# Mixers of a two-layer hybrid trunk in another order: mLSTM beside the later projections, attention last and alone

## The chip, the cores and the metric

The kernel runs on one core of one Trainium2 chip. The metric is the device time of one launch in microseconds (us). Three runs of the kernel before gave a median of 1076.05 us (1075.78 to 1082.33).

## The reference, cut to what matters

Two layers (DEPTH = 2) over x of 512 rows and D_MODEL = 1024. In each layer three mixers read one input projection, their heads go side by side through one output projection, and a normalisation and a mixture of experts follow:

```
p = einsum('bsd,dc->bsc', x, w_in[l])
(c_q, c_kv, k_r, m_q, m_k, m_v, m_o, m_g, s_z, s_xbc, s_dt) = _split(p, IN_SIZES)
y_a = _mla(c_q, c_kv, k_r, ...)               # 8 heads: softmax(q k^T) v, latents of 256 and 128
y_b = _mlstm(m_q, m_k, m_v, m_o, m_g, ...)    # 4 heads of 64, both directions, then a norm and an output gate
y_c = _ssd(s_z, s_xbc, s_dt, ...)             # 4 heads of 64, state 128, both directions
heads = concatenate([y_a, y_b, y_c], -1)      # 512 + 256 + 256 columns
x = _layernorm(ALPHA * x + heads @ w_out[l], ...)
x = _layernorm(ALPHA * x + _hier_moe(x, ...), ...)   # 16 experts, group top-1, expert top-2
```

mLSTM's end is `hn = (h - mu) * rsqrt(var + 1e-5) * norm_g` over each head's 64 columns, times `sigmoid(o)`. The three mixers do not need each other; the output projection needs all three.

## The kernel before, in words

**Numbers.** Products run as three matmuls of split operands (`mm3`: high by high, high by low, low by high). x lies transposed in SBUF (`xt`), 8 blocks of 128 columns; the mixers' finished heads are written back into the same blocks (`finish_heads`, an ACTIVATE and a DVE operation on `xt`): attention into blocks 0 to 3, mLSTM 4 and 5, SSD 6 and 7.

**Stages of one layer.** Layer 0 takes about 60 to 285 us for the mixers, layer 1 about 591 to 815 us.
- `ssd()` (the letter d, 19 steps): the SSD's scans on 128-row chunks; `ssd_heads()` (h) its heads.
- `projections()` (p, 12 steps): the input projection's blocks for mLSTM q and k, then the two attention latents (`cqb`, `ckb`), then mLSTM v (`mvb`) and the output gate (`tho`). Their weights are loaded in the order of `todo_w` (L715), two blocks ahead.
- `mla_in()` (i): norms of the latents, v of attention.
- `mlstm()` (m, 16 steps): four heads in two pairs; products of 130 and 65 columns; at the end, all on the vector engine DVE, mean (`mu`), difference, variance (`va`), a reciprocal root of 16 columns by some 14 small operations (`rq_*`), two 1024-column products and two 512-column products with the gate; then eight 128x128 transposes into banks 3 and 4 and the heads into `xt`. This end is called the mLSTM's tail below.
- `attention()`: generators `scores` (s, 5 steps a head) and `values` (v). A score tile is three matmuls of 512 columns into one bank, a DVE maximum (`mx`), an ACT exponential with its sum (`sums`), a DVE reciprocal and a normalisation (L1337; on POOL for heads 0 to 5, on DVE for 6 and 7). `values` transposes four 128x128 blocks into one bank, copies them out, and multiplies with v (64 x 512 outputs).

**What sets the order.** The string `SEQ` (L72), one letter a step, says which generator takes its next step (the loop at L1393). The order in which instructions are written in this way is their priority; a scheduler then moves each engine's instructions within it as operands come free, and the queue of every engine runs in the order so fixed. In SEQ before, SSD and nearly all the projections come first, then mLSTM steps are spread among the steps of attention, to about its fifth head.

**PSUM.** Eight banks of 512 columns. The mixers use three pools: PA (banks 0 to 2, attention's keys, queries and outputs), PM (banks 3, 4, mLSTM) and PT_ (banks 5 to 7, score tiles and transposes, and mLSTM's edge products).

**After the mixers.** The output projection (`wout`, L1688 to L1760) multiplies `xt` blocks in the order SSD, mLSTM, attention, with pools P4 and P5 of PSUM banks (L1403); its first four outputs lie in P4's four banks. Its weights are loaded by `wo_load` on SP's queue and split by `wo_split` (ACT, and a subtraction on POOL, L409).

Nearly every operation is recorded at L229, a wrapper of the engines; so the rows are told apart by tile names: b are PSUM banks, s SBUF slots, xt the transposed input or heads, ident the identity of a transpose.

Of the kernel before, what the change touches and what calls it, by code (L numbers as in the profile page):

```python
# [13 lines left out]
AF = mybir.ActivationFunctionType  # L14
# [6 lines left out]
NT = S // 128  # L21
# [47 lines left out]
MA = 3  # L69
NM = 2  # L70
SSD_STEPS = 19
SEQ = 'dpddpdpdpddpdddpdpddpiddpidpiddpddphimmssmsmssmsvmsvvsmsvsmsmvssvsvvsvmmvsvsvsmvmsvsmsvmsvsvmvvsvmmsvsvsmssvvmsmsvsvmsvsvsvvssvsvvsvsvvvvvv'  # L72

ROPE_INV = [1.0, 0.5623413324356079, 0.3162277638912201, 0.17782793939113617, 0.10000000149011612,
            0.05623413249850273, 0.03162277489900589, 0.017782794311642647, 0.009999999776482582,
# [110 lines left out]
class Buf:  # L186
# [4 lines left out]
    def free(self):  # L191
        assert self.live
        self.live = False
        self.pool.put(self)
# [17 lines left out]
def tile_trunk(ctx: ExitStack, tc: tile.TileContext, ins, out, dbg=None, depth=DEPTH):  # L212
# [22 lines left out]
    V, A, G, T = Pinned(nc.vector, "V"), Pinned(nc.scalar, "A"), nc.gpsimd, Pinned(nc.tensor, "T")  # L235
# [13 lines left out]
    Q, R = View(pool, F32R), View(pool, F32)  # L249
    banks = [psp.tile([128, 512], F32, name=f"b{i}") for i in range(8)]  # L250
# [8 lines left out]
    def ph(n):  # L259
        if PHASE:  # L260
            PHASE(n)
            if n != lastp[0]:
                lows[lastp[0]] = [min(a, b.low) for a, b in zip(lows.get(lastp[0], [99] * 4), (pool, PA, PB))]
                pool.low, PA.low, PB.low = len(pool.whole), 9, 9
            if n == "comb":
                print(lows)
            lastp[0] = n
# [28 lines left out]
    def win_load(l, c0, n):  # L296
        raw = []
        for q in range(2):
            b = R.get_half(4 * n) if n <= 128 else R.get(4 * n)
            load(b.ap, ins["w_inp"], l * D * IN_P + D * WIN_AT[c0] + q * 128 * 4 * n, [[4 * n, 128], [1, 4 * n]])  # L300
            raw.append(b)
        return raw

    def win_split(raw, a, n, keep=False, eng=()):
        res = []
        for i, b in enumerate(raw):
            h, lo = (Q.get_half(4 * n) if n <= 128 else Q.get(4 * n, keep=keep) for _ in range(2))
            split(h.v("p (k c) -> p k c", k=4), lo.v("p (k c) -> p k c", k=4),
                  b.v("p (k c) -> p k c", k=4)[:, :, a:a + n], G if i in eng else V)
            res.append((h, lo))  # L310
        return res
# [95 lines left out]
    def split(dst_h, dst_l, src, eng=V):  # L407
        r = A.activation(dst_h, src, AF.Copy)
        eng.tensor_sub(dst_l, src, dst_h.bitcast(F32))  # L409
        return r  # L410
# [9 lines left out]
    def mm3(p, ah, al, bh, bl, start=True, stop=True):  # L420
        T.matmul(p, ah, bh, start=start, stop=False)
        T.matmul(p, ah, bl, start=False, stop=False)
        T.matmul(p, al, bh, start=False, stop=stop)
# [134 lines left out]
    for l in range(depth):  # L558
# [50 lines left out]
        def kpart(w, k, c0, m, n):  # L609
            h, lo = w[k // 4]  # L610
            a = (k % 4) * n + c0
            return h.ap[:, a:a + m], lo.ap[:, a:a + m]
# [9 lines left out]
        def proj_fm(w, c0, m, n=256):  # L622
            p = PA.get()
            proj_part(p, lambda k: kpart(w, k, c0, m, n))
            return p

        def proj_tm(w, i, n=256):
            p = PA.get(n)
            s = slice(i * 128, (i + 1) * 128)
            for k in range(KD):  # L630
                h, lo = kpart(w, k, 0, n, n)
                mm3(p.ap, xh[k][:, s], xl[k][:, s], h, lo, start=(k == 0), stop=(k == KD - 1))
            return p
# [78 lines left out]
        ph("gates")  # L712
        sp = aa = em = sb = kra = rows = wx = None

        todo_w = [(c0, 256) for c0 in (1968, 1712, 416, 672, 0)] + [(256, 128), (928, 256), (1184, 256)]  # L715
        raw_w = []

        def win_next():

            while todo_w and len(raw_w) <= AHEAD:  # L720
                raw_w.append(win_load(l, *todo_w.pop(0)))
            return raw_w.pop(0)
# [260 lines left out]
        def ssd_heads():  # L983
            for g in range(2):
                finish_heads(6 + g, yz[g].ap)
                yz[g].free()
            yield


        mq, mk, mvb, tho, cqb, ckb = [], [], [], [], [], []  # L990

        def projections():
            for dst in (mq, mk):
                r = win_next()
                w = win_split(r, 0, 256)
                free(r)
                for g in range(2):
                    p = proj_fm(w, g * 128, 128)
                    b = R.get_half()
                    A.activation(b.ap, p.ap, AF.Copy, scale=1.0 if dst is mq else 0.125)  # L1000
                    if dst is mq:

                        b = [b]
                        for e in range(2):
                            z = R.get_half()
                            G.memset(z[64 - 64 * e:128 - 64 * e], 0.0)
                            V.tensor_copy(z[64 * e:64 * e + 64], p[64 * e:64 * e + 64])
                            b.append(z)
                    dst.append(b)
                    p.free()  # L1010
                    yield
                free(*w)
            r = win_next()
            w = win_split(r, 0, 256)
            free(r)
            r = win_next()
            w1 = win_split(r, 0, 128)
            free(r)
            for ww, c0, n, dst in ((w, 0, 256, cqb), (w, 128, 256, cqb), (w1, 0, 128, ckb)):
                p = proj_fm(ww, c0, 128, n)  # L1020
                q = R.get_half()
                if dst is cqb:
                    c = Q.get()
                    h, lo = c.ap[:, 0:512], c.ap[:, 512:1024]
                    sc = pt[:, len(cqb), 6:7]
                    A.activation(h, p.ap, AF.Identity, scale=sc)
                    V.scalar_tensor_tensor(lo, p.ap, sc, h.bitcast(F32), op0=OP.mult, op1=OP.subtract)
                    c = (c, h, lo)
                else:
                    c = R.get_half()  # L1030
                    A.activation(c.ap, p.ap, AF.Copy)
                A.activation(q.ap, p.ap, AF.Square)
                p.free()
                dst.append((c, q))
                yield
            free(*w, *w1)
            r = win_next()
            w = win_split(r, 0, 256)
            free(r)
            mvb.append(R.get(1040))  # L1040
            mv1 = mvb[0].v("p (i h c) -> p i h c", i=NT, h=4)
            V.memset(mv1[:, :, :, 64:65], 1.0)
            for i in range(NT):
                p = proj_tm(w, i)
                A.activation(mv1[:, i, :, 0:64], p.v("p (h c) -> p h c", h=4), AF.Copy)
                p.free()
                if i % 2:
                    yield
            free(*w)
            r = win_next()  # L1050
            w = win_split(r, 0, 256)
            free(r)
            for i in range(NT):
                p = proj_tm(w, i)
                if i % 2 == 0:
                    tho.append(R.get_half())
                A.activation(tho[-1][:, (i % 2) * 256:(i % 2) * 256 + 256], p.ap, AF.Tanh, scale=0.5)
                p.free()
                if i % 2:
                    yield  # L1060
            free(*w)
# [318 lines left out]
        def mix(*parts):  # L1380

            live = [[0, n, nme, g] for n, nme, g in parts]
            while live:
# [3 lines left out]
                if next(t[3], 1):  # L1387
                    live.remove(t)
                    if PHASE:
                        print(t[2], "steps", t[0] - 1, "of", t[1])  # L1390

        streams = {"d": ssd(), "p": projections(), "m": mlstm(), "i": mla_in(), "h": ssd_heads()}
        for n, t in enumerate(SEQ):  # L1393
            ph({"m": "mlstm", "d": "ssd", "p": "proj"}.get(t, "attn"))
# [5 lines left out]
        free([b for b, _, _ in kb], [b for b, _, _ in mla["qn"]], mla["kn"][0], mla["uk"][0], mla["vt"])  # L1400


        P4, P5 = Slots(banks[0:4], 512), Slots(banks[4:8], 512)  # L1403


        class Expert:
# [243 lines left out]
        def wo_split(raw, n):  # L1650
            h, lo = Q.get(1024, full=True), Q.get(1024, full=True)
            split(h.ap, lo.ap, raw.ap, G if n in WOG else V)
            raw.free()
            return h, lo
# [34 lines left out]
        for a, q in enumerate(order):  # L1689
            w = wo_split(raws[0][a], a)  # L1690
# [124 lines left out]
        for c in WSEQ.split():  # L1815
            if c[0] == "Z":
                i = int(c[1])
# [411 lines left out]
```

## Time and profile before

| | |
|---|---|
| median of 3 runs | 1076.05 us |
| profiled execution | 1076.42 us |
| its span | 1074.7 us |
| mean granted clock of TensorE | 0.971 |
| PE busy | 999.9 us, 93% |
| DVE busy | 834.5 us, 78% |
| ACT busy | 645.0 us, 60% |
| POOL busy | 273.7 us, 25% |

PE is the matmul engine, PEld its weight loads, DVE the vector engine, ACT the scalar engine, POOL GpSimd, SP the engine that issues DMAs. Busy time is summed over an engine's instructions. Times inside the profile count from the span's start; the profiled execution lasted 1.7 us longer than its span. The two layers repeat the same stretches with an offset of about 530 us. A granted clock of 1.00 is 2.4 GHz, 0.50 is 1.2 GHz.

### The profile page before, as it was taken

What the parts mean: (1) busy time and instruction counts of PE and PEld (TensorE: products, weight loads), DVE (VectorE), ACT (ScalarE), POOL (GpSimd) and SP (SyncE); (2) the same over time, 40 slices, a digit from 0 to 9 for tenths busy, and PEclk for the clock granted to TensorE, in tenths of its full rate; (3) what the DMA queues carried; (4) which work ended last, traced back from release to release, by engine and by line L of the source; (5) the groups of instructions that cost most, each with busy time, mean ns of one, the idle gap of its engine ahead of it and who ended that gap; (6) DMA issues with size and microseconds to landing.
All of it is one profiled execution on the core that took longest, in us unless ns stands there. A gap on an engine that the chain in (4) does not pass through costs nothing. (4 is left out here: it accounts for less than half of the span.)

```text
span 1074.7 us, 15552 instructions
## 1 busy us (share of the span) xinstructions
PE 999.9 (93%) x5310; PEld 741.5 (69%) x5310; DVE 834.5 (78%) x1830; ACT 645.0 (60%) x1182; POOL 273.7 (25%) x234
## 2 busy tenths in 40 slices
PE   6999999979998899999999999989799979999995
PEld 6876787546688666666698768866467866666653
DVE  8995558787648699999969946577875677999996
ACT  5565546646423588888645564566463327878874
POOL 1000002322004155566000000023210322655652
PEclk9999999999997899999999999999899988999998
DMA  7211100133646789995632120012347477999833
GB/s 303 69 51 39 40 21 26 54 118 129 233 157 236 265 280 346 339 340 179 212 125 70 40 68 1 21 40 62 115 156 268 147 275 223 310 341 344 299 80 155
DMA packets 51795, 176.76 MB, mean 164 GB/s; under 512 B 8169, under 2 KB 8681, under 8 KB 51712
## 3 DMA queue, kind: packets, MB, share of 16 engines
q1 hardware_dynamic: 45216, 160.42, 41.9%
q0 software_dynamic: 6496, 15.31, 6.1%
q8 instruction: 42, 0.69, 0.3%
q14 instruction: 41, 0.34, 0.1%
HBM read 159.61 MB, written 23.59 MB: 170 GB/s over the span
## 5 line engine op out<-in xcount | busy, mean ns | idle before, releaser
L229 PE MATMUL b<-s,s 128*128 128x512 f32 (+9 forms) x1262 | 318.9, 404 | 15.5 <-DVE s L229 8.2
L229 PE MATMUL b<-xt,s 128*128 128x512 f32 (+3 forms) x1354 | 295.2, 363 | 12.4 <-ACT s L229 8.8
L229 DVE TENSOR_TENSOR s<-s,s 128x1024 fp32r<-128x1024 f32 (+5 forms) x256 | 250.5, 1004 | 50.1 <-ACT s L229 41.6
L229 ACT ACTIVATE s<-s 128x1024 fp32r<-128x1024 f32 (+6 forms) x242 | 213.4, 924 | 85.0 <-DVE s L229 31.7
L229 PEld LDWEIGHTS b<-xt,s 128*128 128x128 f32 (+2 forms) x1354 | 213.6, 185 | 70.4 <-issue 11.3
L229 PE MATMUL b<-s,xt 128*128 128x256 f32 (+2 forms) x1096 | 255.3, 365 | 0.4 <-POOL s L1522 0.4
L229 PEld LDWEIGHTS b<-s,s 128*128 128x128 f32 (+3 forms) x1262 | 177.2, 173 | 98.3 <-DVE s L229 25.8
L229 ACT ACTIVATE s<-b 128x512 f32<-128x512 f32 (+7 forms) x266 | 128.4, 497 | 173.4 <-PE b L229 164.9
L229 PEld LDWEIGHTS b<-s,xt 128*128 128x128 f32 (+1 forms) x1096 | 172.1, 184 | 44.4 <-issue 4.8
L229 PE MATMUL b<-ident,s 128*128 128x128 f32 (+3 forms) x736 | 109.2, 277 | 25.5 <-DMA s<-x1d,slx 8.8
L229 PEld LDWEIGHTS b<-ident,s 128*128 128x128 f32 (+3 forms) x736 | 82.7, 155 | 59.7 <-ACT s L229 13.9
L229 ACT ACTIVATE xt<-s 128x1024 fp32r<-128x1024 f32 (+1 forms) x84 | 86.3, 1036 | 23.8 <-PE b L229 14.5
L229 DVE TENSOR_TENSOR xt<-s,xt 128x512 fp32r<-128x512 f32 (+1 forms) x76 | 79.7, 1053 | 14.2 <-ACT xt L229 14.0
L1597 POOL DMA_INDIRECT acc<-s,slx x28 | 53.1, 1896 | 103.1 <-ACT s L229 100.6
L229 ACT ACTIVATE s<-b,mx,qsc 128x512 f32<-128x512 f32 x64 | 49.8, 784 | 25.4 <-DVE mx L229 25.1
L1337 POOL TENSOR_SCALAR s<-s,sums 128x512 f32<-128x512 f32 x48 | 37.6, 790 | 105.1 <-DVE sums L229 93.0
L1445 POOL DMA_INDIRECT s<-x1d,slx x30 | 44.3, 1477 | 64.6 <-PE b L229 28.2
L229 PE MATMUL b<-xt 128*96 128x512 f32 x184 | 58.3, 402 | 0.0
L1093 POOL MEMSET s<- 128x780 f32 x4 | 3.0, 755 | 215.7 <-DVE s L229 182.0
L229 DVE TENSOR_REDUCE mx<-b 128x1 f32<-128x512 f32 x64 | 43.2, 686 | 17.4 <-PE b L229 17.1
L229 ACT ACTIVATE xt<-b 128x384 fp32r<-128x384 f32 (+1 forms) x72 | 33.8, 518 | 36.7 <-PE b L229 36.5
L229 ACT ACTIVATE s<-b,slw 96x512 f32<-96x512 f32 (+1 forms) x60 | 39.1, 682 | 18.3 <-PE b L229 12.5
(255 smaller groups left out, 1056.6 us busy)
## 6 DMA issues: line engine op xcount, KB each, us to landing
s<-in_w_gu_dram SPq DMA_DIRECT2D x128, 512.0 KB, 8.3
s<-in_expert_w_down_dram SPq DMA_DIRECT2D x64, 512.0 KB, 8.2
s<-in_w_inp_dram SPq DMA_DIRECT2D x36, 512.0 KB, 4.5
s<-in_w_outp_dram SPq DMA_DIRECT2D x16, 512.0 KB, 4.4
x1d<-s SPq DMA_DIRECT2D x8, 512.0 KB, 2.9
acc<-s SPq DMA_DIRECT2D x8, 512.0 KB, 4.0
s<-acc SPq DMA_DIRECT2D x8, 512.0 KB, 6.9
s<-in_x_t_dram SPq DMA_DIRECT2D x4, 512.0 KB, 5.4
```

The source lines that it names most:

```text
L229: r = f(*a, **kw)
L1093: G.memset(cb.ap, 0.0)
L1337: (V if hd in NORMV else G).tensor_scalar(P.ap, P.ap, sums, 0.0, op0=OP.mult, op1=OP.add)
L1445: self.ga = G.indirect_dma_start(out=self.xg[:BLK], out_offset=None, in_=x1d[0:128 * n, :], in_offset=bass.IndirectOffsetOnAxis(ap=ix[:BLK ...
L1597: G.indirect_dma_start(out=acc[:, :], out_offset=bass.IndirectOffsetOnAxis(ap=self.ix[:BLK, 0:1], axis=0), in_=yt[:BLK], in_offset=None, b ...
```

## The change

`SEQ` is rewritten: all SSD steps come first, with six of the twelve projection steps; then the mLSTM with the other six projection steps and `mla_in`; the mLSTM's last four steps stand among the first five score steps; the rest of attention follows with nothing beside it. For this the mLSTM v projection moves ahead of the latents, in the code and in the order of the weight loads. P4 and P5 name the banks in another order, so that the first outputs of the output projection lie in banks 3 and 4. No instruction is added or taken away: PE has the same 5154 in both.

```
-SEQ = 'dpddpdpdpddpdddpdpddpiddpidpiddpddphimmssmsmssmsvmsvvsmsvsmsmvssvsvvsvmmvsvsvsmvmsvsmsvmsvsvmvvsvmmsvsvsmssvvmsmsvsvmsvsvsvvssvsvvsvsvvvvvv'
+SEQ = ('dpdddpdddpdddpdddpdddpddd' 'mpmmpmmmpimmpmmipmmi' 'smsmhsmsms'
+       + 'sv' * 35 + 'v' * 5)
...
-        todo_w = [(c0, 256) for c0 in (1968, 1712, 416, 672, 0)] + [(256, 128), (928, 256), (1184, 256)]
+        todo_w = [(c0, 256) for c0 in (1968, 1712, 416, 672, 928, 0)] + [(256, 128), (1184, 256)]
...
         def projections():
...
+            mvb.append(R.get(1040))
+            mv1 = mvb[0].v("p (i h c) -> p i h c", i=NT, h=4)
+            V.memset(mv1[:, :, :, 64:65], 1.0)
+            for i in range(NT):
+                p = proj_tm(w, i)
+                A.activation(mv1[:, i, :, 0:64], p.v("p (h c) -> p h c", h=4), AF.Copy)
+                p.free()
+                if i % 2:
+                    yield
+            free(*w)
+            r = win_next()
+            w = win_split(r, 0, 256)
+            free(r)
             r = win_next()
             w1 = win_split(r, 0, 128)
...
-        P4, P5 = Slots(banks[0:4], 512), Slots(banks[4:8], 512)
+        P4, P5 = Slots(banks[3:5] + banks[0:2], 512), Slots(banks[5:8] + banks[2:3], 512)
```

(The same v block is taken out behind the latents.)

**First place: PE, layer 0, from the mLSTM's last transposes to the first matmul of the output projection.** b_72 and b_73 are banks 3 and 4, b_74 to b_76 banks 5 to 7, b_71 bank 2. Before, the transposes into b_72 and b_73 and then:

```order
L229 MATMUL b_72<-ident,s_159_1610 128x128 x2
L229 MATMUL b_73<-ident,s_159_1610 128x128 x2
L229 MATMUL b_72<-ident,s_159_1610 128x128 x2
L229 MATMUL b_73<-ident,s_159_1610 128x128 x2
L229 MATMUL b_71<-s_116_1071,s_217_2103 128x512 x3
L229 MATMUL b_71<-s_120_1137,s_218_2106 128x512 x3
L229 MATMUL b_72<-s_281_2542,xt 128x512
L229 MATMUL b_74<-s_135_1278,s_235_2266 128x512 x2
L229 MATMUL b_75<-s_135_1278,s_235_2266 128x512 x2
```

After, the mLSTM's last transposes:

```order
L230 MATMUL b_76<-ident,s_207_1997 128x128
L230 MATMUL b_72<-ident,s_129_1299 128x128 x2
L230 MATMUL b_73<-ident,s_129_1299 128x128 x2
L230 MATMUL b_75<-ident,s_96_929 128x128
L230 MATMUL b_72<-ident,s_129_1299 128x128 x2
L230 MATMUL b_73<-ident,s_129_1299 128x128 x2
L230 MATMUL b_75<-ident,s_201_1965 128x128
```

and, further on, the first matmuls of the output projection:

```order
L230 MATMUL b_75<-ident,s_212_2040 128x128
L230 MATMUL b_75<-ident,s_248_2295 128x128
L230 MATMUL b_75<-ident,s_251_2311 128x128
L230 MATMUL b_72<-s_293_2554,xt 128x512
L230 MATMUL b_73<-s_293_2554,xt 128x512
L230 MATMUL b_71<-s_139_1355,s_233_2177 128x512 x3
L230 MATMUL b_71<-s_143_1417,s_234_2180 128x512
```

Before, six matmuls stand between the mLSTM's last transposes and the first matmul of the output projection (`s,xt`, 128x512). After, 146 instructions of attention stand between them: 69 products of 512 columns, 61 transposes and 16 products with v. Ahead of the last product with v stand 44 matmuls of the output projection before and 31 after.

**Second place: DVE, layer 0, the beginning of the mLSTM's tail.** mu, va and the slot s_159 (before) or s_129 (after) are the tail; mx and sums belong to attention. Before:

```order
L229 TENSOR_TENSOR s_159_1610<-s_159_1610,s_184_1793 128x4x128
L229 TENSOR_REDUCE mu_2181<-s_159_1610 128x16
L229 TENSOR_REDUCE mx_2169<-b_76 128x1
L229 TENSOR_SCALAR mu_2181<-mu_2181 128x16
L229 COPY s_184_1793<-b_75 128x512
L229 TENSOR_SCALAR mx_2169<-mx_2169,qsc_1307 128x1
L229 TENSOR_TENSOR s_159_1610<-s_159_1610,mu_2181 128x1024
L229 TENSOR_TENSOR xt<-b_70,xt 128x512
L229 RECIPROCAL sums_2172<-sums_2172 128x1
L229 TENSOR_REDUCE mx_2231<-b_76 128x1
L229 TENSOR_REDUCE va_2187<-s_226_2185 128x16
```

After:

```order
L230 TENSOR_TENSOR s_198_1941<-s_96_929,s_198_1941 128x512
L230 TENSOR_REDUCE mu_1886<-s_129_1299 128x16
L230 RECIPROCAL sums_1930<-sums_1930 128x1
L230 TENSOR_TENSOR s_147_1478<-b_69,s_147_1478 64x512
L230 TENSOR_SCALAR mu_1886<-mu_1886 128x16
L230 TENSOR_TENSOR s_146_1473<-b_70,s_146_1473 64x512
L230 TENSOR_TENSOR s_129_1299<-s_129_1299,mu_1886 128x1024
L230 TENSOR_REDUCE mx_1954<-b_74 128x1
L230 TENSOR_REDUCE mx_1970<-b_76 128x1
L230 TENSOR_REDUCE va_1892<-s_191_1890 128x16
```

From the mean's reduction to the last gate product DVE works through the same 24 operations of the tail in both; between them, and some rows on either side, stand attention's operations of its fifth head and later before, of its first three heads after.

**Third place: PE, layer 0, the mLSTM's products of 65 columns.** Before, they stand among transposes and score tiles of attention:

```order
L229 MATMUL b_73<-s_133_1221,s_174_1720 128x65
L229 MATMUL b_74<-s_133_1221,s_174_1720 128x65
L229 MATMUL b_75<-s_135_1278,s_177_1745 128x512 x3
L229 MATMUL b_76<-s_135_1278,s_177_1745 128x512 x3
L229 MATMUL b_72<-s_161_1624,s_89_854 128x130 x3
L229 MATMUL b_73<-s_133_1221,s_90_858 128x65
L229 MATMUL b_73<-s_133_1221,s_176_1732 128x65
```

After, those of the first pair of heads stand among products of the input projection (`s,xt`, 128x256):

```order
L230 MATMUL b_70<-s_162_1585,xt 128x256 x2
L230 MATMUL b_70<-s_163_1586,xt 128x256
L230 MATMUL b_70<-s_162_1585,xt 128x256
L230 MATMUL b_71<-s_160_1581,xt 128x256
L230 MATMUL b_71<-s_161_1582,xt 128x256
L230 MATMUL b_73<-s_120_1116,s_107_1023 128x65
L230 MATMUL b_73<-s_120_1116,s_144_1428 128x65
```

Those of the second pair's second direction stand, after, ahead of the first score tiles.

## Rows read from the trace of the kernel before

**Rows 1.** The page: busy time of each engine, share of the span, instructions.
```profile
PE 999.9 (93%) x5310; PEld 741.5 (69%) x5310; DVE 834.5 (78%) x1830; ACT 645.0 (60%) x1182; POOL 273.7 (25%) x234
```

**Rows 2.** Mixers by stretch: us, busy and count per engine, clock, DMA share, GB/s.
```profile
45.00:60.00 15.00, 14.80 (x69) 11.63 (x68) 13.32 (x59) 5.98 (x10) 1.56 (x3) 1.00 0.12 38
60.00:171.00 111.00, 109.93 (x609) 85.34 (x608) 71.27 (x161) 60.66 (x149) 1.51 (x2) 1.00 0.10 32
...
171.00:222.00 51.00, 48.41 (x272) 34.32 (x270) 40.58 (x113) 33.05 (x89) 16.42 (x24) 1.00 0.17 53
222.00:248.00 26.00, 19.91 (x79) 11.04 (x78) 21.66 (x53) 12.13 (x22) 7.03 (x5) 0.87 0.33 109
248.00:285.00 37.00, 35.97 (x172) 22.90 (x171) 26.11 (x59) 23.23 (x44) 5.16 (x5) 1.00 0.47 160
...
701.00:752.00 51.00, 47.14 (x263) 33.16 (x261) 39.10 (x109) 32.80 (x88) 16.31 (x24) 1.00 0.17 53
752.00:778.00 26.00, 19.89 (x82) 10.98 (x81) 21.59 (x53) 12.34 (x22) 7.06 (x5) 0.87 0.31 106
```

**Rows 3.** The mLSTM's tail by stretch, layer 0, its whole in layer 1 second.
```profile
225.80:244.40 18.60, 12.51 (x44) 5.59 (x41) 16.76 (x44) 8.64 (x16) 4.66 (x4) 0.89 0.26 90
756.00:774.60 18.60, 12.49 (x44) 5.59 (x41) 16.72 (x43) 8.64 (x16) 4.67 (x4) 0.86 0.25 90
...
240.40:246.20 5.80, 5.33 (x15) 2.91 (x16) 4.49 (x9) 2.69 (x4) 1.68 (x2) 0.50 0.00 0
```

**Rows 4.** PE in time: start, us, operation, count, [idle before <- what ended it].
```profile
225.42 2.67 PE L229 MATMUL b<-s,s 128*64 128x512 f32 x10
227.93 0.60 PE L229 MATMUL b<-ident,s 128*128 128x128 f32 x4
228.28 4.09 PE L229 MATMUL b<-s,s 128*128 128x512 f32 x12
...
233.82 1.43 PE L229 MATMUL b<-s,s 128*128 128x512 f32 x5 [1.19 <-ACT s L229]
...
237.72 0.44 PE L229 MATMUL b<-ident,s 128*128 128x128 f32 x2 [2.12 <-ACT s L229]
240.35 1.35 PE L229 MATMUL b<-ident,s 128*128 128x128 f32 x4 [2.20 <-POOL s L1337]
...
260.22 5.07 PE L229 MATMUL b<-s,s 128*128 128x512 f32 x21
```

**Rows 5.** DVE in time, the tail's reductions, 226 to 237 us.
```profile
225.81 0.55 DVE L229 TENSOR_TENSOR s<-s,b 128x390 f32<-128x390 f32 x1
...
228.76 1.22 DVE L229 TENSOR_REDUCE mu<-s 128x16 f32<-128x1024 f32 x1
229.89 0.68 DVE L229 TENSOR_REDUCE mx<-b 128x1 f32<-128x512 f32 x1
...
235.43 1.21 DVE L229 TENSOR_REDUCE va<-s 128x16 f32<-128x1024 f32 x1
```

**Rows 6.** Groups by form, 60 to 285 us: busy, mean ns, idle before, releaser.
```profile
L229 ACT ACTIVATE s<-b,mx,qsc 128x512 f32<-128x512 f32 x32 | 25.0, 783 | 12.9 <-DVE mx L229 12.8
L229 DVE TENSOR_REDUCE mx<-b 128x1 f32<-128x512 f32 x32 | 21.6, 686 | 8.7 <-PE b L229 8.5
L1337 POOL TENSOR_SCALAR s<-s,sums 128x512 f32<-128x512 f32 x24 | 18.8, 790 | 44.9 <-DVE sums L229 39.3 <-DVE dn L229 5.6
L229 DVE TENSOR_TENSOR s<-s,s 128x512 fp32r<-128x512 f32 x18 | 12.5, 699 | 4.3 <-ACT s L229 4.2
L229 ACT ACTIVATE s<-s 128x512 fp32r<-128x512 f32 x18 | 11.3, 633 | 8.3 <-DMA s<-in_w_inp_dram 3.8 <-DVE s L229 2.2 <-POOL s L1337 1.6
L229 DVE TENSOR_SCALAR mx<-mx,qsc 128x1 f32<-128x1 f32 x32 | 6.1, 206 | 0.1
L229 DVE TENSOR_TENSOR s<-b,rot 128x512 f32<-128x512 f32 x8 | 5.5, 681 | 0.4 <-PE b L229 0.4
L229 DVE RECIPROCAL sums<-sums 128x1 f32<-128x1 f32 x32 | 5.1, 158 | 4.7 <-ACT s L229 4.4
```

**Rows 7.** Groups by form, PE, 222 to 285 us.
```profile
L229 PE MATMUL b<-ident,s 128*128 128x128 f32 x84 | 15.9, 301 | 5.3 <-POOL s L1337 3.2 <-ACT s L229 2.1
L229 PE MATMUL b<-s,xt 128*128 128x512 f32 x44 | 14.1, 420 | 0.0
```

**Rows 8.** Groups by form, 60 to 171 us: projections on PE, weight splits on DVE.
```profile
L229 PE MATMUL b<-xt,s 128*128 128x512 f32 x192 | 49.6, 402 | 0.0
L229 PE MATMUL b<-s,xt 128*128 128x256 f32 x192 | 24.6, 284 | 0.0
...
L229 DVE TENSOR_TENSOR s<-s,s 128x1024 fp32r<-128x1024 f32 x8 | 9.8, 1224 | 6.3 <-ACT s L229 3.5 <-PE b L229 2.8
```

**Rows 9.** A stretch behind the mixers, 340 to 380 us.
```profile
340.00:380.00 40.00, 35.43 (x196) 27.22 (x196) 27.94 (x91) 19.39 (x30) 8.80 (x7) 0.83 0.79 255
```

More of the change, by code (lines that the diff above doesn't have):

```diff
@@ L1036, in projections @@
             free(*w, *w1)
[L1037 to L1049, printed above, removed]
             r = win_next()
```

## The prediction

> **What bounds it now.** I read the page first: PE is busy 93% of the span, DVE 78% [rows 1], so a gain can only come out of PE's idle time, and a loss out of work that PE used to do while attention waited. Then the mixers by stretch, where the change works. Up to 171 us PE idles 1.3 us of 126, though DVE is busy 89% in the first 15 us; from 171 to 222 us, attention with mLSTM among it, it idles 2.6 us (layer 1: 3.9); from 222 to 248 us it idles 6.1 us of 26 at a granted clock of 0.87; after that, with the output projection among attention, 1.0 us of 37 [rows 2]. Then the one poor stretch by itself: 225.8 to 244.4 us, from the mLSTM's last additions to its last gate product. DVE is busy 16.8 of 18.6 us, PE 12.5, and in the 5.8 us behind its middle the clock is 0.50, that is 1.2 GHz [rows 3]. Last PE in time there: it waits 1.2, 2.1 and 2.2 us for ACT and for POOL's normalisation [rows 4], and what keeps these late stands in DVE's queue: a maximum of attention begins behind the tail's 1.22 us reduction, with a second one for the variance further on [rows 5]. I call this the seam. Layer 1 has the same one [rows 3].
>
> The terms below are per layer, against the profiled execution's 1076.42 us (median of the runs: 1076.05, 0.4 less).
>
> **Term 1, the seam: +2.** The mLSTM's tail isn't made shorter, and it isn't moved out of attention: DVE's order has it among the maxima and sums of heads 0 to 2, where it stood among those of head 4 and on (second place). Counted from the tail's mean to its last gate product, the order puts 51 DVE instructions there after and 43 before: five more of 512 columns and three more maxima (8 x 0.69 = 5.5 us), two more small ones (0.4), one fewer of 1024 (1.22) and one fewer of 390 (0.55) [rows 5, 6]; that makes +4.1 us. On PE the same piece has 52 instructions for 39: eight more of 512 columns (0.24 each, 5.07/21), ten more transposes (0.13), five fewer products with v (0.50) [rows 4], +0.7 us. A transpose takes 0.09 us where four follow one another without a gap (227.93 to 228.28) [rows 4] and 0.19 by its group's busy time [rows 7]; I take the middle. A product with v counts as two rows of the trace: ten rows in 2.51 us are five of 0.50 [rows 4]. If DVE sets the pace, as its 90% says, PE idles up to 3.4 us longer (upper end). The lower end is that the seam's idle time goes altogether, -6.1. I take +2, near the upper end, because the row of the same work shows DVE nearly full.
>
> **Term 2, mLSTM beside projections: -3.2.** Its products of 65 and 130 columns wait on ACT and DVE; now matmuls of the input projection, which need nothing but weights, stand between them (third place). That a projection fills such gaps shows in the stretch up to 171 us. The idle time of the stretch with both mixers, 2.6 and 3.9 us, mean 3.2, goes [rows 2]. Ends: 0 and -3.9.
>
> **Term 3, attention alone: +6.** The 146 instructions of the first place are PE's work with nothing beside it: 69 x 0.24 + 61 x 0.13 + 16 x 0.50 = 32.5 us. Before, output projection stood among such work: 44 of its matmuls from 222 us on [rows 7]; just behind the mLSTM's end, the order has 16 of them, 16 x 0.24 = 3.8 us, to about 12.3 us of attention, 0.31. Does attention by itself keep PE busy? One head costs PE 12 score matmuls, 7.5 for query and key, 16 transposes, 4 products with v: 19.5 x 0.24 + 16 x 0.13 + 4 x 0.50 = 8.8 us. It costs DVE four maxima, scalings and reciprocals, 4 x (0.69 + 0.21 + 0.16) = 4.2, the rotary product 0.68, two splittings of 0.70, a copy-out and half a head's end near 0.69 and 0.35 [rows 6]: 7.3 us, 83% of PE's. The chain behind a score tile is 0.69 + 0.21 + 0.78 + 0.16 + 0.79 = 2.6 us until it may be transposed, that behind a query 0.68 + 0.63 + 0.70 = 2.0 us [rows 6], and eight tiles a head, scores and transposes, turn through three banks (5 to 7). So the chains fit, but with little over. Two rows have DVE as dense: 80% with PE 5% idle from 171 to 222 us, and 83% with PE 23% idle from 222 to 248 us [rows 2]. By the first attention alone would lose 1.7 us, by the second 7.5; if all the waits that output projection fills now come out, 0.31 x 32.5 = 10. I take +6, the middle of the outer two, since every row of attention has other work beside it. Ends: 0 and +10.
>
> **Term 4, SSD with fewer projections: +1.** From 60 to 171 us DVE works 71.3 us of 111 [rows 2]. Latents and output gate leave that stretch: 72 x 49.6/192 + 96 x 24.6/192 = 18.6 + 12.3 = 30.9 us of PE, and on DVE four splittings of weights, 4 x 1.22 = 4.9 us [rows 8]. 66 us of DVE's work then lie beside 80 of PE's, 83%. At 89% PE idles 0.2 us of 15 and at 80% 2.6 of 51 [rows 2], so the ends are 1 and 4 us of 80. I take +1, since the first row is SSD work as here.
>
> **Term 5, clock and the rest: 0.** The stretch at 0.50 costs 2.9 us now (half of 5.8) [rows 3]; the seam that stays keeps it. Ends -2.9 (it goes) and, below, a loss. The output projection's start: its first banks are free earlier, but its first matmul stands 146 instructions behind the mLSTM's transposes where it stood six behind, and its work on PE is the same; the weights come behind four expert loads in SP's queue and have the 32.5 us of attention to land and to be split, POOL being at 25% [rows 1]. That cover gone, one load would show at the projection's start, and no row of the mixers shows such a wait. The weights of v come one block earlier, those of the query latent one later, two blocks ahead as before.
>
> **Sum:** +2 - 3.2 + 6 + 1 + 0 = +5.8 per layer, 11.6 for two: 1076.4 + 11.6 = **1088 us**. Terms 1 and 3 move together, as both ask how dense DVE is; their likely spread (+-2.5 a layer) gives 1083 to 1093.
>
> **Rivals.**
>
> *Attention alone is enough for PE, and the seam closes (other side).* The tail now lies at attention's beginning, beside the keys' and queries' first products, and may be passed there without holding a score tile. Then the seam's 6.1 us and its clock's 2.9 go, Term 2 goes, and attention alone and SSD cost 4 and 1: -6.1 - 2.9 - 3.2 + 4 + 1 = -7.2, twice is -14.4: **1062 us**. For it: the projections beside mLSTM and PE at 97% from 248 us on. Against it: DVE's order, with more attention between the tail's steps than before. It decides if PE idles under 2 us from the tail's mean to its last gate product. Chance 0.25.
>
> *It only moves.* Seam as before (0), Term 2 gained, and attention alone waits as in the nearest rows, near +3, SSD +1: +0.8 a layer, **1078 us**. This is also the case that the new banks do nothing: they are handed over early and used 146 instructions later. For it: the same instructions on all engines. Chance 0.25.
>
> *The clock falls in attention alone.* From 340 to 380 us PE works 35.4 of 40 us, with gaps, at a clock of 0.83 [rows 9]. At that level the 32.5 us would take 32.5 x (1/0.83 - 1) = 6.7 us more: +12.5 a layer, **1101 us**. Against it: from 171 to 222 and 701 to 752 us PE is busy 95 and 92% with gaps, in attention on the same three banks, and the granted clock is 1.00 [rows 2]. The Trainium skill (TensorE: Matmul & The Clock Gate, "A second HAM failure mode: psum-queue depth-cycling") says that a kernel that cycles through PSUM banks can idle so often for so short a time between groups of matmuls that the clock swings between its levels. By that page these three banks would suffer it; the two rows at 1.00 disagree so far, but show no attention without a filler, so a small chance stays. Chance 0.08.
>
> My forecast has the rest, 0.42.
>
> **Numbers.** About 1% (10.8 us, so 1065.3 and 1086.8) is what a measurement of this kernel tells from no change. Forecast, 0.42: two thirds above 1086.8, one third within. Rival 1: five sixths below 1065.3. Rival 2: within, but for 0.02 above. Rival 3: above. Faster 0.21, slower 0.28 + 0.02 + 0.08 = 0.38, same 0.41. Range: 1062 to 1100 leaves out half of rival 1's chance, half of rival 3's and tails of 0.03, 2 in 10.
>
> **What would show it.** Term 1: DVE around 90% busy from the tail's mean to the last gate product, and PE idle 6 to 9 us there; below 2 us, rival 1 holds. Term 2: PE over 98% busy where 65-column products stand beside `s,xt` 128x256. Term 3: between the mLSTM's transposes and the first output projection PE idle some 15 to 20% of about 39 us, ended by ACT, DVE or POOL's normalisation; idle under 5% refutes it. Term 4: the SSD's stretch some 31 us shorter, with PE idle about 1 us. Term 5: a clock below 1.00 in attention alone would be rival 3; a wait of the first output projection for a load or for POOL would refute the zero.

## The result, and the profile after

The changed kernel takes 1086.85 us (median of 20 runs, 1079.51 to 1094.01); the kernel before, run beside it, 1077.12 us (20 runs). The ratio is 1.0082, 95% interval 1.0064 to 1.0100: **slower by 0.8%**, where 1.1% was forecast (1088 us). The profiled execution's span is 1084.1 us, 9.4 more than before.

The head of the page of the changed kernel:

```profile
span 1084.1 us, 15564 instructions
PE 1005.7 (93%) x5310; PEld 737.6 (68%) x5310; DVE 835.6 (77%) x1830; ACT 644.1 (59%) x1182; POOL 272.2 (25%) x234
```

Of the 9.4 us PE idles 3.6 (78.4 for 74.8) and is busy 5.8 longer, with the same 5310 recorded matmuls [rows 1]. The ends of matmuls are modelled in these records, so a short wait between two of them lies inside busy time; idle time by itself is not the whole loss. Nor is the clock: its mean over the execution is 0.975, where it was 0.971.

Where it came up shows in two places of PE's time that both kernels have: the router's last product behind each layer's mixers, and the transposes at the beginning of layer 1. Before (start, us, operation, count):

```profile
339.94 0.99 PE L229 MATMUL b<-wrg,s 128*128 128x20 f32 x8
535.73 1.60 PE L229 MATMUL b<-ident,s 128*128 128x128 f32 x12 [0.16 <-DVE s L229]
869.48 0.99 PE L229 MATMUL b<-wrg,s 128*128 128x20 f32 x8
```

After:

```profile
345.74 0.99 PE L230 MATMUL b<-wrg,s 128*128 128x20 f32 x8
540.29 1.60 PE L230 MATMUL b<-ident,s 128*128 128x128 f32 x12 [0.21 <-DVE s L230]
877.54 0.99 PE L230 MATMUL b<-wrg,s 128*128 128x20 f32 x8
```

The mixers and the output projection cost 5.8 us more in layer 0 and 3.5 more in layer 1 (8.06 less 4.56); the experts differ by -1.2 and +1.3, though nothing was changed there.

The mixers by stretch, after (stretch, us, busy and count of PE, PEld, DVE, ACT, POOL; granted clock, DMA share, GB/s): SSD with six projection steps; mLSTM with the other five (the new order has eleven letters p); the first score tiles; the mLSTM's tail, from its mean to its last gate product; attention to its last product with v; then the last two in layer 1.

```profile
60.00:135.00 75.00, 74.28 (x381) 52.99 (x380) 55.58 (x110) 49.09 (x123) 1.51 (x2) 1.00 0.16 57
135.00:188.00 53.00, 52.44 (x332) 47.36 (x331) 30.55 (x94) 23.44 (x65) 5.78 (x8) 0.94 0.17 61
188.00:199.10 11.10, 9.53 (x59) 7.94 (x58) 9.34 (x33) 4.79 (x10) 1.80 (x3) 1.00 0.00 1
199.10:215.60 16.50, 13.03 (x49) 7.39 (x49) 15.93 (x43) 8.15 (x18) 4.66 (x6) 0.79 0.29 95
215.60:289.20 73.60, 68.49 (x303) 38.08 (x301) 46.04 (x108) 41.72 (x86) 17.23 (x18) 1.00 0.20 71
729.20:745.30 16.10, 12.11 (x49) 6.88 (x49) 15.91 (x42) 8.27 (x18) 4.70 (x6) 0.89 0.29 97
745.30:819.00 73.70, 68.58 (x303) 38.14 (x301) 47.31 (x109) 42.70 (x87) 17.22 (x18) 1.00 0.21 70
```

Tail and attention of before, cut by the same instructions, layer 0 and layer 1:

```profile
228.70:244.40 15.70, 9.61 (x30) 3.68 (x29) 13.96 (x33) 7.64 (x14) 4.22 (x4) 0.87 0.20 68
244.40:285.10 40.70, 39.67 (x187) 26.18 (x185) 28.43 (x63) 25.66 (x48) 7.53 (x6) 0.97 0.44 152
759.00:774.60 15.60, 9.49 (x29) 3.58 (x28) 13.89 (x32) 7.52 (x14) 4.13 (x4) 0.83 0.20 68
774.60:814.80 40.20, 39.14 (x187) 25.57 (x185) 28.37 (x63) 25.61 (x48) 7.56 (x6) 0.98 0.47 153
```

In the tail PE idles 3.5 us (layer 1: 4.0), where it was 6.1. Behind the tail it idles 5.1 us of 73.6 or 73.7, where it was 1.0 and 1.1 of some 40. In layer 0 DVE is busy only 63% there (46.0 of 73.6), and the clock is 1.00. What PE waits for behind the tail, in total (us, times, longest), layer 0, after:

```profile
PE b L230 <- POOL s L1338: 2.4, 4, 1.3
PE b L230 <- ACT s L230: 1.4, 3, 0.7
PE b L230 <- POOL s L410: 0.7, 1, 0.7
PE b L230 <- DVE s L230: 0.5, 1, 0.5
```

The first is the normalisation of P, which the transposes wait for; the third is the splitting of the output projection's weights, whose first share stands on POOL behind all the normalisations (POOL begins it at 263.67 us, after 4.75 us in which it idles and waits for ACT's half of the split).

### The profile page after: what moved, and what is told of

It reads as the page before. It is cut to its first block, busy times and chain, and to the rows that moved or that the text cites. A ratio compares the mean times of both kernels' runs of the same rounds, so it can differ in the third digit from the quotient of the medians.

```text
span 1084.1 us, 15564 instructions
## 1 busy us (share of the span) xinstructions
PE 1005.7 (93%) x5310; PEld 737.6 (68%) x5310; DVE 835.6 (77%) x1830; ACT 644.1 (59%) x1182; POOL 272.2 (25%) x234
## 5 line engine op out<-in xcount | busy, mean ns | idle before, releaser
L230 PE MATMUL b<-s,s 128*128 128x512 f32 (+10 forms) x1270 | 334.3, 412 | 11.3 <-DVE s L230 7.3
L230 PE MATMUL b<-xt,s 128*128 128x512 f32 (+3 forms) x1354 | 298.2, 364 | 12.2 <-ACT s L230 8.7
L230 DVE TENSOR_TENSOR s<-s,s 128x1024 fp32r<-128x1024 f32 (+6 forms) x258 | 248.7, 989 | 37.7 <-ACT s L230 35.9
L230 ACT ACTIVATE s<-s 128x1024 fp32r<-128x1024 f32 (+7 forms) x242 | 213.3, 923 | 80.3 <-DVE s L230 50.5
L230 PE MATMUL b<-s,xt 128*128 128x256 f32 (+2 forms) x1096 | 258.5, 368 | 1.9 <-POOL s L410 1.5
L230 PEld LDWEIGHTS b<-s,xt 128*128 128x128 f32 (+1 forms) x1096 | 174.4, 184 | 46.9 <-issue 6.3
L230 PE MATMUL b<-ident,s 128*128 128x128 f32 (+3 forms) x736 | 105.9, 274 | 30.4 <-DMA s<-x1d,slx 12.1
L230 PEld LDWEIGHTS b<-ident,s 128*128 128x128 f32 (+3 forms) x736 | 80.3, 153 | 65.6 <-POOL s L1338 20.4
L230 DVE TENSOR_TENSOR xt<-s,xt 128x512 fp32r<-128x512 f32 (+1 forms) x76 | 81.5, 1077 | 24.4 <-ACT xt L230 24.1
L1446 POOL DMA_INDIRECT s<-x1d,slx x30 | 40.3, 1345 | 57.8 <-DVE slw L230 22.3
L1523 POOL TENSOR_TENSOR xt<-s,xt 128x512 fp32r<-128x512 f32 x32 | 44.1, 1398 | 5.4 <-ACT xt L230 4.6
```

The source lines that it names most:

```text
L230: r = f(*a, **kw)
L1446: self.ga = G.indirect_dma_start(out=self.xg[:BLK], out_offset=None, in_=x1d[0:128 * n, :], in_offset=bass.IndirectOffsetOnAxis(ap=ix[:BLK ...
L1523: G.tensor_sub(lo[:, 512:1024], src[:, 512:1024], h[:, 512:1024].bitcast(F32))
```

## The experiments

Theory A: attention alone waits on the chain behind its score tiles, which mLSTM and output projection used to cover; the new banks buy nothing. Rival B: the banks and the output projection's start cost the time. Rival C: three PSUM banks for scores and transposes hold attention back. All ratios are to runs of the kernel before taken beside the experiment, so they need not be the ratio of the medians named here.

**One part alone.** The changed kernel with the old pools, `P4, P5 = Slots(banks[0:4], 512), Slots(banks[4:8], 512)`:

> The new order of the mixers with P4 and P5 in their old banks. Theory A (the time went into the order: attention with no other work beside it waits, and the new banks buy nothing): 1.006 to 1.010 of the kernel before, as the whole change. Rival B (the banks and the start of the output projection cost the time): 1.003 or less.

Measured: 1081.76 us, ratio 1.0039 (1.0017 to 1.0060). Between the two: the order makes about half of the loss, and in this order the banks make the rest. The kernel before with the new pools:

> The old order with P4 and P5 in the new banks. Theory A: 0.998 to 1.002 of the kernel before. Rival B: 1.005 or more.

Measured: 1076.92 us, 0.9999 (0.9975 to 1.0022). The banks cost something only together with the new order; neither theory had that. Whether it is the place of the first outputs:

```
-        P4, P5 = Slots(banks[3:5] + banks[0:2], 512), Slots(banks[5:8] + banks[2:3], 512)
+        P4, P5 = Slots(banks[0:2] + banks[3:5], 512), Slots(banks[5:8] + banks[2:3], 512)
```

> The changed kernel with the output projection's first outputs in banks 0 and 1 and the next in 3 and 4 (P4 = banks 0, 1, 3, 4), P5 as in the changed kernel. The new order with both old pools came to 1.0039, the whole change to 1.0082. If the first outputs' place in the mLSTM's banks costs the difference: 1.002 to 1.006. If it is P5 without bank 4: 1.007 to 1.010.

Measured: 1091.94 us, 1.0108 (1.0081 to 1.0134). The first outputs' place in banks 3 and 4 isn't it. What is left is that banks 2 and 4 change places between the two pools; which pool it is wasn't tested. Attention behind the tail takes 72.4 us with the old pools and 73.6 with the new:

```profile
215.50:287.90 72.40, 67.64 (x305) 38.63 (x304) 46.70 (x107) 41.36 (x86) 17.43 (x18) 1.00 0.21 72
```

That is 1.2 us a layer of the 2.3 that the ratios differ by (0.43% of 1077 us, two layers). It lies in the products with v. From the start of one row to its end, or to the start of PE's next row where that comes first, such a row takes 305 ns before and 306 in the new order with the old pools, but 326 with the new pools; in the old order with the new pools it is 305 again (means of layer 0, worked out from the starts in the traces, stretches of low clock left out). Some 62 rows at 20 ns are the 1.2 us. Another 0.5 lies behind attention: the router's last product starts at 343.92 us here and at 345.74 in the changed kernel. Why a pool that is used later lengthens these products isn't shown.

**Banks of attention.** In the changed kernel:

```
+        PT5, mdone = Slots(banks[5:8] + banks[3:5], 512), []
...
-                    pS = PT_.get()
+                    pS = (PT5 if mdone else PT_).get()
...
-                    pb = PT_.get()
+                    pb = (PT5 if mdone else PT_).get()
```

(`mdone` is filled at the end of `mlstm()`.)

> The changed kernel, but once the mLSTM is done attention's score tiles and transposes turn through five PSUM banks (5 to 7, 3 and 4) and not through three. Rival C (three banks hold attention back when it stands alone): PE's 5.1 us of idle time a layer behind the mLSTM's last gate product fall under 2, and the ratio to before falls to 0.999 to 1.003. Theory A (it is the chain maximum, exponential, sum, normalisation on POOL that isn't covered): idle time 3.5 us or more, 1.005 to 1.010.

Measured: 1086.88 us, 1.0094 (1.0060 to 1.0129). By time and idle time this is what Theory A expected, but it doesn't decide against Rival C. Its last two stretches, tail and attention:

```profile
196.00:211.10 15.10, 8.27 (x23) 4.43 (x24) 10.30 (x28) 3.77 (x7) 2.47 (x2) 0.55 0.10 36
211.10:283.10 72.00, 68.00 (x315) 42.30 (x314) 52.22 (x121) 47.03 (x97) 17.83 (x21) 0.95 0.27 90
```

Idle time in attention is still 4.0 us, and in the tail it rises to 6.8, at a clock of 0.55. Two of PE's rows show that this kernel differs in more than the number of banks:

```profile
209.70 1.97 PE L230 MATMUL b<-ident,s 128*128 128x128 f32 x8 [2.42 <-DVE s L230]
212.81 1.11 PE L230 MATMUL b<-ident,s 128*128 128x128 f32 x4 [1.14 <-DVE xt L230]
```

The first are the mLSTM's eight transposes, which wait for the tail's gate products; the second, attention's, wait until DVE has carried the mLSTM's heads out of banks 3 and 4. So attention's next tiles were tied to the end of the tail: PE has only 23 rows beside it, where the changed kernel has 49. The granted clock of the seven runs is 0.956 to 0.965; that of the changed kernel's 20 is 0.966 to 0.982. An upper estimate of what low clock costs is the span times what the clock lacks of 1: 41 us a run here (mean), 29 in the changed kernel. So this kernel loses up to 12 us more to the clock and takes the same time; without that part the means are 1047 us before, 1058 for the changed kernel and 1047 here. (Among the changed kernel's 20 runs, 1 us more of this estimate goes with 0.7 us more time; at that rate the 12 us stand for some 8.) And a row of a product with v takes 284 ns here, for 326. These figures speak for Rival C. It stays open, as no kernel was run that gives attention more banks without tying it to the tail.

**Other work beside attention.** A generator for the first two shares of the output projection, as a letter w in the order (its helpers move ahead of the loop):

```
-SEQ = (... 'smsmhsmsms' + 'sv' * 35 + 'v' * 5)
+SEQ = (... 'smswmhsmsms' + 'sv' * 8 + ('svsvsvwsv') * 4 + 'sv' * 11 + 'v' * 5)
...
+        def wout_head():
+            raw0.extend(wo_load(0, q) for q in order[:2])
+            yield
+            ps.extend(P4.get() for _ in range(2))
+            for a, q in enumerate(order[:2]):
+                w = wo_split(raw0[a], a)
+                wo0.append(w)
+                for i in range(2):
+                    wo_mm(ps[i], i, q, w, a == 0, False)
+                    yield
```

> The changed kernel with the first 24 matmuls a layer of the output projection (SSD and mLSTM heads, into banks 3 and 4) written among the steps of attention, so that its heads have 5.8 us of other PE work beside them. Theory A: PE's idle time behind the mLSTM's last gate product falls from 5.1 us a layer to 1 to 3, and the ratio to before to 1.000 to 1.005. Rival C (banks): they only move, 1.006 to 1.010, idle time 4 us or more.

Measured: 1075.64 us, 0.9980 (0.9954 to 1.0007): the whole loss is back, a little more than expected. Tail and attention, layer 0, and what PE still waits for in the second:

```profile
195.80:212.60 16.80, 12.10 (x51) 6.58 (x52) 14.97 (x40) 9.87 (x20) 5.20 (x6) 1.00 0.01 1
212.60:285.30 72.70, 71.54 (x324) 42.30 (x323) 49.16 (x110) 41.07 (x85) 14.60 (x17) 1.00 0.30 102
```

```profile
PE b L229 <- DVE s L229: 0.7, 1, 0.7
PE b L229 <- POOL s L1337: 0.3, 1, 0.3
```

Idle time in attention is 1.2 us for 5.1, in less time and with 21 more matmuls in it. Without the clock's part, estimated as above, its runs have a mean of 1049 us. Since this kernel keeps the new order, attention without cover is the cause of the loss, and the cover is what brings it back. A row of a product with v takes 329 ns here too, so the cover hides the cost of the banks and doesn't take it away. Whether the early banks are needed for it was not tested.

**The chain itself.** In the changed kernel, and as a control in the kernel before:

```
-                    (V if hd in NORMV else G).tensor_scalar(P.ap, P.ap, sums, 0.0, op0=OP.mult, op1=OP.add)
+                    if hd in NORMV:
+                        V.tensor_scalar(P.ap, P.ap, sums, 0.0, op0=OP.mult, op1=OP.add)
```

> The changed kernel without POOL's normalisation of P (heads 0 to 5 leave it out; heads 6 and 7 keep theirs on DVE). Theory A: the chain from a score tile to its transposes is shorter by 0.8 us and one engine, and its waits are uncovered in attention alone, so idle time behind the gate falls from 5.1 us a layer to 1 to 3 and the ratio to 0.997 to 1.004. Rival (the chain is covered, PE waits for DVE's order): idle time 4 us or more, 1.006 to 1.010.

Measured: 1071.33 us, 0.9942 (0.9915 to 0.9969), further down than expected.

> The kernel before without POOL's normalisation of P in heads 0 to 5, the control of the same cut in the changed kernel, which came to 0.9942 of before, 1.4 of a hundred less than the changed kernel. Theory A (the chain is uncovered in attention alone and was covered by mLSTM and output projection): 0.993 to 0.999, a gain of at most half of 1.4. Rival (the chain costs as much wherever attention stands): 0.984 to 0.988.

Measured: 1072.69 us, 0.9936 (0.9917 to 0.9955). The same cut gives 1.40% in the changed kernel and 0.64% before; without it the two kernels take the same time. The difference, 0.76% or 8 us (some 0.4% either way by the intervals), is as much as the whole loss of the change: the chain's 0.8 us on POOL was about half covered and is not now. A rival, that POOL's work slows down DVE's, doesn't show: DVE is busy 46.5 us in attention without the normalisation and 46.0 with it. The attention of the changed kernel without it (the tail ends at 211.1):

```profile
211.10:278.20 67.10, 65.49 (x293) 36.87 (x292) 46.51 (x108) 41.69 (x85) 4.74 (x2) 1.00 0.24 85
```

It takes 6.5 us less than 73.6. Of these 3.5 were idle time; PE is also busy 3.0 less, but with ten rows fewer in the stretch (293 for 303), so what the chain costs inside busy time isn't shown by it. PE's wait of 0.7 us for POOL's splitting is gone too, so the cut takes out a little more than the chain.

**The seam.** Out of `mlstm()`, in both kernels, come the lines from `mu = small([128, 16], tag="mu")` up to the loop with the gate.

> The kernel before without the mLSTM's normalisation (mean, difference, variance, root and its product are left out; the gate and the transposes stay). Measures what the seam is worth where it stood. From the trace of before: 6.1 us of PE's idle time and 1.8 us of low clock a layer, so 10 to 16 us less, 0.985 to 0.991.

Measured: 1064.81 us, 0.9881 (0.9850 to 0.9913).

> The changed kernel without the mLSTM's normalisation, as in the run on before. Term 1 as it was predicted (the seam costs 2 us a layer more at attention's beginning): this gains 14 to 20 us on the changed kernel, 0.990 to 0.995 of before. Corrected theory (the seam costs 2 to 3 us less there, as the idle times of the two traces say): it gains 5 to 11 us, 0.998 to 1.004.

Measured: 1080.22 us, 0.9996 (0.9970 to 1.0021). The tail is worth 12.8 us before and 9.3 after (0.86% of 1.0082 to 0.9996), 4.6 a layer. The 14 to 20 of Term 1 as predicted are refuted. That it is cheaper after than before, by 3.5 us in all, lies within what these intervals allow for no difference; the two traces' idle times say the same direction (3.5 and 4.0 for 6.1). The granted clock rises without the tail in both kernels, in the mean of the runs from 0.971 to 0.978 before and from 0.973 to 0.976 after, so the tail's worth isn't PE's idle time alone.

**More of the same.** 36 matmuls instead of 24 (`order[:3]`), with all splittings on DVE (`WOG = ()`), and with POOL's kept:

> As the run with fillers, with 36 matmuls a layer written among the steps of attention instead of 24 (the first attention heads' share too) and all four splittings of the output projection's weights on DVE. Theory A: idle time in attention 1 us or less a layer, 0.994 to 0.999 of before. If DVE becomes the bound by the splittings moved to it: 0.999 to 1.003.

Measured: 1078.38 us, 0.9993 (0.9967 to 1.0020).

> As the run with 24 fillers, with 36 a layer (the first attention heads' share too), the splittings of weights left where they are (two on POOL). If more cover helps: 0.994 to 0.998. If the 24 have filled what there is to fill and POOL's splittings now stand in the normalisations' way: 0.997 to 1.003.

Measured: 1081.81 us, 1.0036 (1.0011 to 1.0060). More cover than 24 is no gain, in the places where it stands here (the two orders differ a little). The 24 with the tail's step later (`'smswhsmsms' + 'sv' * 8 + 'm' + ...`):

> As the run with 24 fillers a layer, and with the mLSTM's last step eight score steps later, so that attention's maxima stand ahead of the tail in DVE's queue. Theory A with what is left in the seam (5 us of idle time a layer with fillers): the seam's idle time falls by 1 to 3 us, 0.993 to 0.998 of before. If the tail takes the same place in DVE's time whatever its priority: 0.996 to 1.001.

Measured: 1076.33 us, 0.9980 (0.9955 to 1.0005), as without. No kernel here is shown to beat the kernel before; the two at 0.998 come nearest, and beat the changed one by 1%.

## Why the prediction was right, point by point

**The sum** was 11.6 us; the medians differ by 9.7. Sign and place held. That the size came out so near is in part luck: the order, which the terms priced, made 0.39% by itself (4.2 us) with the old pools, and the other half came from the banks, which Term 5 put at nothing. Terms 1 and 2 were off as well, in opposite directions: by idle time Term 1 was some 4 us a layer too high, Term 2 some 2 too low.

**Term 3, attention alone, +6 a layer: right in place and about in size.** It is the one term that decides. Between the tail and the last product with v PE idles 5.1 us for 1.0, so +4.1 by idle time. Cover brings back 1.0% (5.5 us a layer). The sign that was named, PE idle 15 to 20% of about 39 us from the mLSTM's transposes to the first output projection, came out at half of that: 3.7 of 40.5 us, 9%, still over the 5% that would have refuted the term.

```profile
216.60:257.09 40.49, 36.76 (x160) 19.91 (x158) 25.16 (x63) 23.97 (x53) 11.57 (x15) 1.00 0.25 92
```

The work priced at 32.5 us was busy 36.8: part of the loss lies inside busy time, as in the products with v above. (The 7.5 us by the second dense row should have been 9.9, as the row idles 6.1 us for 19.9 of PE's work; the sum doesn't use it.) The step's reasoning was wrong in one place: it asked how dense DVE is and priced the waits by DVE's 80 to 83%. DVE was at 63%. What PE waited for was the end of one chain through four engines, at POOL in 2.4 of the 5.1 us; the sum that said it fits (2.6 us) left out that the scheduler had nothing else to put there. How much of the loss belongs to the chain's length and how much to the three banks that its tiles turn through is open.

**Term 1, the seam, +2: wrong.** The step that failed is "if DVE sets the pace, PE idles up to 3.4 us longer". DVE is denser than before (15.9 of 16.5 us, 97%, for 89%), the stretch is 0.8 us longer in layer 0 and 0.5 in layer 1, and yet PE idles 2.6 and 2.1 us less. In layer 0 a lower clock (0.79 for 0.87) keeps PE busy for longer; in layer 1 the clock is higher (0.89 for 0.83), so it isn't that alone. PE has 49 rows in the tail for 30 and 29: the added DVE work was attention's own and came with work for PE. More work of attention among the tail's steps was more for PE to do, not more to wait for.

**Term 2, -3.2: half right.** Beside projections PE idles 0.6 us of 53, as predicted. But 1.6 us came back in the 11 us between there and the tail, where the second pair's last products stand with the first score tiles, so 2.1 us are left of 2.6 (layer 1: 2.2 of 3.9), and not nothing. Terms 1 and 2 together were -1.2; by idle time they measure -3.1 in layer 0 (8.7 to 5.6) and -3.8 in layer 1 (10.0 to 6.2).

**Term 4, +1: not seen.** PE idles 0.7 us of 75 with SSD, at DVE 74%.

**Term 5, 0: wrong in two points.** The loads hid. The splitting on POOL did not: PE waits 0.7 us for it in each layer, the wait that was named as what would refute the zero. With the old pools in the new order PE has no such wait. And the banks, whose only effect in the term was to be free earlier, cost 0.4% in this order and nothing in the old one, half of the whole loss.

**The rivals.** The seam did not close (3.5 us, not under 2), so the other side is out. That it only moves, 1078 us, is out by the interval. The clock in attention alone is 1.00 in both layers, though PE waits there again and again between groups of matmuls in three PSUM banks: what the Trainium skill (TensorE: Matmul & The Clock Gate, "A second HAM failure mode: psum-queue depth-cycling") warns of does not show in this profile.

## What to carry to other kernels

Where two streams share an engine, ask of each what it would do by itself before they are parted: the chain from a product to the next product that reads it, in microseconds, against the other work that stands beside it, and how many buffers its tiles turn through. An engine far from full can still end the longest waits (POOL here, busy 17.2 of 73.6 us). Buffers that were handed over early gained nothing here, where the instructions that use them still stood late in the queue. And an experiment that gives a stage more buffers can tie it to the stage that held them: look at what its waits became, and at the clock, before a rival is called out.

## What the runs showed that was not expected

The clock fell where PE did not idle: from 155 to 165 us of the changed kernel, among products of 1, 130 and 256 columns, PE is busy all of the time and the granted clock is 0.58 and 0.74. From 152.5 us on it had done 16 products of one column, eight of 65 and five of 256, with no idle time recorded.

```profile
155.00:160.00 5.00, 5.00 (x28) 5.00 (x28) 2.42 (x21) 0.00 (x0) 0.00 (x0) 0.58 0.00 0
160.00:165.00 5.00, 5.00 (x34) 4.95 (x33) 2.61 (x9) 0.43 (x1) 0.00 (x0) 0.74 0.25 79
```

This costs 3.4 us (5 x 0.42 + 5 x 0.26). The profile of the kernel with fillers doesn't have it at the same instructions; of the ten profiles in the new order five have a drop there, so it seems to come in some executions and not in others. The new order's runs also spread more widely than the old one's (1079.5 to 1094.0 us, against 1074.5 to 1084.9). The time goes with the clock: the fastest of the changed kernel's 20 runs has a mean granted clock of 0.982, the slowest 0.967. What makes the drops come and go was not tested.
